# Dilated attention on one NeuronCore: the modulation's products in groups of four array quarters, and a score pair's two heads in alternation

## The chip, the cores and the metric

The kernel runs on one core of a Trainium2 chip as one program of five engines that run beside each other: TensorE (PE, with its weight loads shown as PEld), VectorE (DVE), ScalarE (ACT), GpSimd (POOL) and SyncE (SP), which here only issues DMA transfers. Each engine works through its own list of instructions in order and waits at semaphores for the others. The metric is the device time of one execution in microseconds (us). An execution that the hardware profiler records is taken apart from the timed ones.

## What is computed

One encoder layer, applied with the same weights to a request of 1024 rows and one of 256 rows (1280 together, model width 1024, all in float32). What matters here, from the reference:

```python
mod = jnp.einsum('bd,de->be', jax.nn.silu(c), ada_w) + ada_b
sh1, sc1, gt1, sh2, sc2, gt2 = jnp.split(mod, 6, axis=-1)
h = rmsnorm(x, norm1_g) * (1 + sc1[:, None]) + sh1[:, None]
z = jnp.einsum('bsd,de->bse', h, w_in)
...
for g, (window, dilation) in enumerate(DIL_CONFIGS):
    o_g, lse_g = dilated_group_attention(qkv[:, :, 0, hs], qkv[:, :, 1, hs], qkv[:, :, 2, hs],
                                         slopes[hs], window, dilation)
```

The modulation is a product of two conditioning vectors (one for each request) of length 1024 with a weight of 1024 x 6144. The dilated attention has three groups of four heads, each head 64 wide.

## The kernel before

The program is built in stages that follow each other: the first third of the modulation and the normalised input (to about 60 us), the products of the input with `w_in` by a seven-product scheme (line 244, to about 395 us), then the stage that the change touches ("c" in the code, about 395 to 794 us), then rope, values and the second branch's output ("psB", to about 890 us), latent attention, the output projections and the feed-forward part. A framework's scheduler decides in which order each engine gets its instructions and where it waits; the source gives it priorities, buffer rings and data flow. A tile with `tag` and `bufs` is a ring: a new tile of that tag waits until the oldest one's last reader is done.

Stage c goes through six steps, one for each pair of heads (two) in each group (three). A step has ten blocks `i` of 128 queries. For each block, `weights(i)` computes the scores of the pair's two heads, head 0 from partitions 0 to 63 of the query and key tiles and head 1 from partitions 64 to 127, each into its own bank of PSUM (`S0`, `S1`). In groups 0 and 1 a number is split in a high and a low part (`qh`, `ql`, `kh`, `kl`) and a score is the sum of three products (lines 823 to 825); in group 2 it is one product (line 827). DVE adds the bias and takes the row's extreme (line 832), ACT exponentiates (837), `outputs(i)` transposes on PE (847), copies, and multiplies with the values (862).

Three generators are woven into the ten blocks. `filler` (`side`) makes the remaining products with `w_in` (line 100), long runs of full-array products that need little of the other engines. `norms` (`side2`) normalises the latents. `modulation` (`side3`) makes the other two thirds of the modulation: eight chunks of 512 columns, each of eight products with contraction 128, 32 output rows (two are used) and 512 columns. Product k of a chunk writes quarter k % 4 of the bank `AD` (`tile_position=(0, 32 * j)`), so the four quarters of the array's columns serve four products. In the trace such a product is two PE rows, since a float32 product is made in two passes:

```python
w = mk(cpl, [P, 512], tag="ad", bufs=3)
nc.sync.dma_start(out=w, in_=ada_w[k * P:(k + 1) * P, 512 * c:512 * c + 512])
nc.tensor.matmul(ps[32 * j:32 * j + 32, :], lhsT=cT[:, k, :], rhs=w, start=(k < 4), stop=(k >= 4), tile_position=(0, 32 * j))
yield
```

The first third of the modulation (`ada_chunk`, line 167) has products of the same shape, issued eight in a row. The value rows of an attention group are loaded by `values` into a ring `v` of `VB` tiles with two blocks each; the next group's first blocks are loaded ahead.

Of the kernel before, what the change touches and what calls it, by code (L numbers as in the profile page):

```python
# [8 lines left out]
F32 = mybir.dt.float32  # L9
F32R = mybir.dt.float32r  # L10
# [6 lines left out]
P = 128  # L17
# [29 lines left out]
def kernel(  # L47
# [258 lines left out]
    def bank(tag, bufs=1):  # L306
        return mk(psC[1], [P, 512], tag=tag, bufs=bufs)
# [191 lines left out]
    close_pool(scm)  # L499


    VB, SB = 9, 7
    ccm = open_pool("c", "left")
    cpl = ccm[1]
    psC = open_pool("psC", space=PSUM)
    cT_, abT_ = mk(cpl, [P, KD, 32]), mk(cpl, [P, 6 * KD])
    nc.vector.tensor_copy(cT_, cT)
    nc.vector.tensor_copy(abT_, abT)
    cT, abT = cT_, abT_

    def cls(ap, g, i):
        if i < NS:
# [123 lines left out]
    def norms():  # L636
# [43 lines left out]
        for c, (c0, n) in enumerate(CH):  # L680
# [10 lines left out]
            nc.sync.dma_start(out=f32(kr_d)[1, 0:32, cs_], in_=f32(lo))  # L691
            yield

    NORM = 0, 1
    def modulation():
        for c in range(4, 12):
            ps = bank("AD")
            for k in range(KD):
                j = k % 4
                w = mk(cpl, [P, 512], tag="ad", bufs=3)  # L700
                nc.sync.dma_start(out=w, in_=ada_w[k * P:(k + 1) * P, 512 * c:512 * c + 512])
                nc.tensor.matmul(ps[32 * j:32 * j + 32, :], lhsT=cT[:, k, :], rhs=w, start=(k < 4), stop=(k >= 4), tile_position=(0, 32 * j))
                yield
            rows = stile()
            nc.scalar.copy(out=rows, in_=ps)
            tp = pp().rearrange("p (b n) -> p b n", b=4)
            for b in range(4):
                nc.tensor.transpose(tp[:, b, :], rows[:, b * P:(b + 1) * P], ident)
            chunk_cols(c, tp)
            yield  # L710
# [76 lines left out]
    for pair, g in steps:  # L787
        split = g < 2
        (qh, ql), (kh, kl) = qk[pair, g]
        nxt = steps.index((pair, g)) + 1  # L790
        more = queries_keys(*steps[nxt], qk[steps[nxt]]) if nxt < len(steps) else last_steps()
        if pair and g < 2:
            values(g + 1, 0, 6)
        if g == 0:
            bt = [mk(cpl, [P, 384], tag="bs", bufs=4) for _ in range(2)]
            for h in range(2):
                nc.sync.dma_start(out=bt[h], in_=bias0[2 * pair + h])
            btab = {0: bt, 1: bt}
        else:
            w = 384 if g == 1 else P  # L800
            btab = {}
            for q, src in enumerate((bias1s, bias1p) if g == 1 else (bias2s, bias2p)):
                if g == 1:
                    btab[q] = [mk(cpl, [P, 384], tag="bs", bufs=4) for _ in range(2)]
                else:
                    both = mk(cpl, [P, 384], tag="bs", bufs=4)
                    btab[q] = [both[:, P * h:P * h + P] for h in range(2)]
                for h in range(2):
                    nc.sync.dma_start(out=btab[q][h][:, 0:w], in_=src[2 * pair + h])
        nt = rtile()  # L810
        stat = mk(cpl, [P, 40], tag="stat", bufs=2)
        vg = vts[g]
        def weights(i):
            w0, o, blocks = window(g, i)
            wn = 256 if split else P
            q0 = P * i
            ps = [bank(f"S{h}") for h in range(2)]
            for h in range(2):
                hs = slice(64 * h, 64 * h + 64)
                dst = ps[h][:, 0:wn]  # L820
                if split:
                    a, b_ = qh[hs, q0:q0 + P], kh[hs, w0:w0 + wn]
                    nc.tensor.matmul(dst, lhsT=a, rhs=b_, start=True, stop=False)
                    nc.tensor.matmul(dst, lhsT=a, rhs=kl[hs, w0:w0 + wn], start=False, stop=False)
                    nc.tensor.matmul(dst, lhsT=ql[hs, q0:q0 + P], rhs=b_, start=False, stop=True)
                else:
                    nc.tensor.matmul(dst, lhsT=qh[hs, q0:q0 + P], rhs=kh[hs, w0:w0 + wn], start=True, stop=True)
            sb = stile()
            for h in range(2):
                bias = btab[0 if i < NS else 1][h]  # L830
                b0 = P - o if split else 0
                nc.vector.tensor_tensor_reduce(
                    out=sb[:, 256 * h:256 * h + wn], in0=ps[h][:, 0:wn], in1=bias[:, b0:b0 + wn],
                    scale=-0.125, scalar=3e38, op0=ALU.add, op1=ALU.min, accum_out=stat[:, 10 * h + i:10 * h + i + 1])
            for h in range(2):
                e = sb[:, 256 * h:256 * h + wn]
                nc.scalar.activation(out=e, in_=e, func=AF.Exp, scale=-1.0, bias=stat[:, 10 * h + i:10 * h + i + 1],
                                     accum_out=stat[:, 20 + 10 * h + i:21 + 10 * h + i])
            return sb, blocks

        def outputs(i, sb, blocks):
            tp = mk(psC[1], [P, 512], tag="PT", bufs=2)
            pt = stile()
            for bi, (b, off, m) in enumerate(blocks):
                for h in range(2):
                    cc = 256 * bi + P * h
                    nc.tensor.transpose(tp[0:m, cc:cc + P], sb[:, 256 * h + off:256 * h + off + m], ident)
            if all(m == P for _, _, m in blocks):
                nn = 256 * len(blocks)
                if i % 2:  # L850
                    nc.vector.tensor_copy(pt[:, 0:nn], tp[:, 0:nn])
                else:
                    nc.scalar.copy(out=pt[:, 0:nn], in_=tp[:, 0:nn])
            else:
                for bi, (b, off, m) in enumerate(blocks):
                    nc.vector.tensor_copy(pt[0:m, 256 * bi:256 * bi + 256], tp[0:m, 256 * bi:256 * bi + 256])
            oo = bank("O")[:, 0:P]
            for bi, (b, off, m) in enumerate(blocks):
                for h in range(2):
                    hs = slice(64 * h, 64 * h + 64)  # L860
                    vc = P * pair + 64 * h
                    nc.tensor.matmul(oo[hs, :], lhsT=vg[b][0:m, vc:vc + 64],
                                     rhs=pt[0:m, 256 * bi + P * h:256 * bi + P * h + P],
                                     start=(bi == 0), stop=(bi == len(blocks) - 1), tile_position=(0, 64 * h))
            if i % 2:
                nc.scalar.copy(out=cls(nt, g, i), in_=oo)
            else:
                nc.vector.tensor_copy(cls(nt, g, i), oo)

        quota = 0.0  # L870
        nxt_w = weights(0)
        for i in range(NT):
            now, nxt_w = nxt_w, weights(i + 1) if i + 1 < NT else None
            for part in range(2):
                quota += SIDE / 20
                while quota >= 1:
                    quota -= 1
                    next(side, None)
                if part == 0:
                    outputs(i, *now)  # L880
                if part == 0 or i % 2:
                    next(side3, None)
            for _ in range(SPEED if nxt == len(steps) else 1):
                next(more, None)
            if steps.index((pair, g)) >= NORM[0]:
                for _ in range(NORM[1]):
                    next(side2, None)
        nts[pair][g] = nt
        ps = pp()
        nc.tensor.transpose(ps[0:40, 0:P], stat, ident)  # L890
        srow = stile()[0:40, 0:P]
        nc.vector.tensor_copy(srow, ps[0:40, 0:P])  # L892
        nc.sync.dma_start(out=st_d[pair, g].rearrange("s h (i q) -> (s h i) q", q=P), in_=srow)
        run(more)
        if pair and g < 2:
            values(g + 1, 6)
    run(side2)
    run(side3)

# [59 lines left out]
    def rope_q(j, w):  # L959

        wh, wl = w
        for c, (c0, n) in enumerate(CH):
            ps = pb()
            mm3(ps[:, 0:n], wh, wl, [t[:, c0:c0 + n] for t in cqH], [t[:, c0:c0 + n] for t in cqL])
            tiles_ = vtile(), vtile(), mk(cpl, [P, 512], F32R, tag="ad", bufs=3), mk(cpl, [P, 512], F32R, tag="qk", bufs=3)
            half = rope(ps[:, 0:n], c, co_t[:, c0:c0 + n], si_t[:, c0:c0 + n], [t[:, 0:n] for t in tiles_])
            yield
            next(half)
            for s, t in enumerate(next(half)):
                nc.scalar.dma_start(out=f32(qr_d)[s, P * j:P * j + P, c0:c0 + n], in_=f32(t))  # L970
# [1000 lines left out]
```

## Time and profile before

| | |
|---|---|
| time, median of 3 runs | 2502.05 us (2501.76 to 2503.14) |
| the profiled execution's own time | 2507.67 us |
| its span in the profile | 2505.9 us |
| PE busy in the span | 2396.6 us (96%) |
| stage c, the six steps | about 417 to 736 us |
| stage c, what is left of the filler, and the merge | about 736 to 794 us |
| PE busy on line 702 | 61.8 us |

The profile gives the start and length of every instruction. PE products are pipelined: the length of one reaches past the start of the next, so what a product costs PE is read from its start to the next one's start, not from its length. The span leaves out 1.8 us of the profiled execution's own time.

### The profile page before, as it was taken

The page shows a single profiled execution, that of the slowest core. Times are in us where ns is not written, and L with a number is a line of the kernel's source. Part 1 is how long each engine was busy: PE and PEld are TensorE (multiplying, and loading weights), DVE is VectorE, ACT ScalarE, POOL GpSimd, SP SyncE. Part 2 cuts the span into 40 slices and gives each one's busy share as a digit, 9 for nine tenths or more (in the row PEclk, how much of TensorE's full clock was granted, in tenths as well). Part 3 has the DMA queues.
Part 4 walks back from the last instruction along what each step waited for, and adds up shares of the span by engine and source line. Part 5 has one row for each costly group of instructions (what it writes and reads, how often), then busy time and mean ns, then how long its engine had stood idle before and what let it go on. Part 6 is the DMA issues. An engine that isn't in the chain of part 4 may idle for free. (4 is left out here: it accounts for less than half of the span.)

```text
span 2505.9 us, 37001 instructions
## 1 busy us (share of the span) xinstructions
PE 2396.6 (96%) x13177; PEld 2006.3 (80%) x13177; DVE 1508.6 (60%) x2469; ACT 1081.3 (43%) x2106; POOL 1114.5 (44%) x802
## 2 busy tenths in 40 slices
PE   7899999999999899999998999988999999999987
PEld 3799997565568777777775778778999999988876
DVE  5733333433444778888888543466665566567768
ACT  4421113544433457777776443343322233254434
POOL 1443331100114336666668442045556555538473
PEclk9999999999989999999999989998999999999999
DMA  7132225556537953333333664332223223267554
GB/s 260 47 132 95 95 93 182 165 177 207 169 98 219 299 178 83 81 91 85 84 96 101 159 203 130 135 110 85 85 92 104 80 80 102 76 230 246 171 188 158
DMA packets 274771, 342.87 MB, mean 137 GB/s; under 512 B 24398, under 2 KB 177759, under 8 KB 274587
## 3 DMA queue, kind: packets, MB, share of 16 engines
q1 hardware_dynamic: 248942, 311.40, 40.3%
q10 hardware_dynamic: 25644, 29.12, 3.3%
q8 instruction: 103, 1.69, 0.3%
q14 instruction: 82, 0.66, 0.1%
HBM read 237.06 MB, written 94.19 MB: 132 GB/s over the span
## 5 line engine op out<-in xcount | busy, mean ns | idle before, releaser
L244 PE MATMUL X<-t,wh 128*128 128x320 f32 x2864 | 540.4, 311 | 9.7 <-ACT wh L230 5.7
L244 PEld LDWEIGHTS X<-t,wh 128*128 128x128 f32 x2864 | 453.0, 189 | 10.6 <-ACT wh L230 5.9
L81 POOL TENSOR_TENSOR pl<-p,ph 128x512 fp32r<-128x512 f32 x224 | 298.0, 1339 | 135.8 <-ACT ph L1127 110.3
L244 PE MATMUL X<-t,wl 128*128 128x320 f32 x1432 | 328.8, 311 | 6.3 <-DVE wl L78 6.3
L244 PEld LDWEIGHTS X<-t,wl 128*128 128x128 f32 x1432 | 241.0, 189 | 7.2 <-DVE wl L78 6.7
L1126 ACT ACTIVATE p<-S 128x512 f32<-128x512 f32 x272 | 163.5, 601 | 104.9 <-issue 39.6
L100 PE MATMUL pp<-t,wh 128*128 128x512 f32 (+3 forms) x672 | 201.7, 381 | 3.7 <-DVE sm L892 3.1
L81 POOL TENSOR_TENSOR wl<-wr,wh 128x512 fp32r<-128x512 f32 (+2 forms) x50 | 62.9, 1258 | 310.7 <-ACT wh L209 281.2
L1108 DVE TENSOR_REDUCE m<-mi 128x1 f32<-128x512 f32 x256 | 174.1, 686 | 34.8 <-PE mi L1107 32.0
L230 ACT CAST wh<-wr 128x512 fp32r<-128x512 f32 x113 | 70.3, 622 | 273.4 <-PE X L244 186.7
L78 DVE TENSOR_TENSOR ut<-X,ut 128x640 f32<-128x640 f32 x126 | 101.6, 821 | 138.4 <-PE X L244 85.8
L81 POOL TENSOR_TENSOR wl<-R,wh 128x512 fp32r<-128x512 f32 x63 | 103.4, 1642 | 145.1 <-ACT wh L230 145.1
L1127 ACT ACTIVATE ph<-S 128x512 fp32r<-128x512 f32 x272 | 162.6, 598 | 1.1 <-issue 0.3
L1796 PE MATMUL Y<-bh,ah 128*128 128x512 f32 x385 | 151.9, 395 | 7.5 <-DVE ut L78 6.6
L100 PEld LDWEIGHTS pp<-t,wh 128*128 128x128 f32 (+1 forms) x672 | 111.7, 185 | 58.0 <-issue 29.7
L1796 PE MATMUL Y<-bl,ah 128*128 128x512 f32 x385 | 152.1, 395 | 6.3 <-POOL bl L81 6.3
L1796 PE MATMUL Y<-bh,al 128*128 128x512 f32 x385 | 151.7, 394 | 0.0
L78 DVE TENSOR_TENSOR wl<-wr,wh 128x512 fp32r<-128x512 f32 x119 | 110.9, 932 | 52.7 <-ACT wh L230 47.7
L244 PE MATMUL X<-R,wh 128*128 128x320 f32 x736 | 138.2, 309 | 0.0
L78 DVE TENSOR_TENSOR pt<-X,pt 128x640 f32<-128x640 f32 x60 | 48.6, 824 | 135.9 <-PE X L244 84.5
L78 DVE TENSOR_TENSOR al<-ar,ah 128x640 fp32r<-128x640 f32 x75 | 89.5, 1195 | 57.0 <-ACT ah L1770 54.1
L100 PE MATMUL pp<-t,wl 128*128 128x512 f32 (+3 forms) x336 | 123.2, 367 | 0.0
(439 smaller groups left out, 5788.9 us busy)
## 6 DMA issues: line engine op xcount, KB each, us to landing
ac_d<-ut SPq DMA_DIRECT2D x77, 320.0 KB
ar<-ac_d SPq DMA_DIRECT2D x75, 320.0 KB
R<-in_w_up_dram SPq DMA_DIRECT2D x84, 256.0 KB
br<-in_w_down_dram SPq DMA_DIRECT2D x77, 256.0 KB
ad<-in_ada_w_dram SPq DMA_DIRECT2D x64, 256.0 KB
wr<-in_w_in_dram SPq DMA_DIRECT2D x48, 256.0 KB
rw<-in_w_in_dram SPq DMA_DIRECT2D x20, 512.0 KB
V<-v_d SPq DMA_DIRECT2D x16, 640.0 KB
```

The lines of the kernel that those rows point to most:

```text
L78: nc.vector.tensor_tensor(out=out, in0=a, in1=b, op=op)
L81: nc.gpsimd.tensor_tensor(out=out, in0=a, in1=b, op=op)
L100: nc.tensor.matmul(ps, lhsT=w[k], rhs=x[k], start=(k == 0 and w is wh and x is xh), stop=(k == n - 1 and w is wl))
L230: nc.scalar.copy(out=h, in_=a)
L244: nc.tensor.matmul(ps[:, z, 0:320], lhsT=a[:, k, :], rhs=b[q][k][:, 320 * z:320 * z + 320], start=(j == 0 and i == 0), stop=(j == n - 1 an ...
L1108: nc.vector.reduce_max(out=m2[:, i, c:c + 1], in_=ps, axis=AX.X)
L1126: nc.scalar.activation(out=p_, in_=ps, func=AF.Exp, scale=MSCALE)
L1127: nc.scalar.activation(out=ph, in_=ps, func=AF.Exp, scale=MSCALE)
L1796: nc.tensor.matmul(ps, lhsT=a[:, P * j:P * j + P], rhs=b, start=(f == 0 and a is ah and b is bh), stop=(f == HF - 1 and a is al))
```

## The change

The eight products of a chunk are now issued in two groups of four: four weight tiles are loaded first, and their four products, one for each quarter of the array's columns, follow each other in the code. The ring `ad` has four buffers instead of three. The score products of a block go term by term, head 0 and head 1 in turn, instead of three terms of head 0 and then three of head 1. Space for the fourth `ad` buffer comes from the ring `v` (8 tiles instead of 9) and from two small copies (`cT_`, `abT_`) that are dropped, the originals being used. Of the next group's value blocks four instead of six are loaded ahead.

```diff
-    VB, SB = 9, 7
+    VB, SB = 8, 7
...
-    cT_, abT_ = mk(cpl, [P, KD, 32]), mk(cpl, [P, 6 * KD])
-    nc.vector.tensor_copy(cT_, cT)
-    nc.vector.tensor_copy(abT_, abT)
-    cT, abT = cT_, abT_
...
+    def ad_tile(dt=F32):
+        return mk(cpl, [P, 512], dt, tag="ad", bufs=AD)
...
+    AD = 4
     def modulation():
         for c in range(4, 12):
-            ps = bank("AD")
+            ps, ws = bank("AD"), []
             for k in range(KD):
                 j = k % 4
-                w = mk(cpl, [P, 512], tag="ad", bufs=3)
+                w = ad_tile()
                 nc.sync.dma_start(out=w, in_=ada_w[k * P:(k + 1) * P, 512 * c:512 * c + 512])
-                nc.tensor.matmul(ps[32 * j:32 * j + 32, :], lhsT=cT[:, k, :], rhs=w, start=(k < 4), stop=(k >= 4), tile_position=(0, 32 * j))
+                ws.append(w)
                 yield
+                if j < 3:
+                    continue
+                for i in range(4):
+                    nc.tensor.matmul(ps[32 * i:32 * i + 32, :], lhsT=cT[:, k - 3 + i, :], rhs=ws.pop(0), start=(k < 4), stop=(k >= 4),
+                                     tile_position=(0, 32 * i))
...
-            values(g + 1, 0, 6)
+            values(g + 1, 0, 4)
...
-            for h in range(2):
-                hs = slice(64 * h, 64 * h + 64)
-                dst = ps[h][:, 0:wn]
-                if split:
-                    a, b_ = qh[hs, q0:q0 + P], kh[hs, w0:w0 + wn]
-                    nc.tensor.matmul(dst, lhsT=a, rhs=b_, start=True, stop=False)
-                    nc.tensor.matmul(dst, lhsT=a, rhs=kl[hs, w0:w0 + wn], start=False, stop=False)
-                    nc.tensor.matmul(dst, lhsT=ql[hs, q0:q0 + P], rhs=b_, start=False, stop=True)
-                else:
-                    nc.tensor.matmul(dst, lhsT=qh[hs, q0:q0 + P], rhs=kh[hs, w0:w0 + wn], start=True, stop=True)
+            terms = ((qh, kh), (qh, kl), (ql, kh)) if split else ((qh, kh),)
+            for t, (a, b_) in enumerate(terms):
+                for h in range(2):
+                    hs = slice(64 * h, 64 * h + 64)
+                    nc.tensor.matmul(ps[h][:, 0:wn], lhsT=a[hs, q0:q0 + P], rhs=b_[hs, w0:w0 + wn], start=(t == 0), stop=(t == len(terms) - 1))
```

How the scheduler sets these instructions is seen in its lists. First PE's list of before, in the first step of group 0, which is the place at which the trace stands at 425.4 us: line 823 to 825 are the three terms, `S_610` is head 0's bank, `S_611` head 1's, `R` the query and key tiles, and line 702 is a modulation product.

```order
L823 MATMUL S_610_3775<-R_3686,R_3672 128x256
L824 MATMUL S_610_3775<-R_3687,R_3672 128x256
L825 MATMUL S_610_3775<-R_3686,R_3673 128x256
L823 MATMUL S_611_3776<-R_3686,R_3672 128x256
L824 MATMUL S_611_3776<-R_3687,R_3672 128x256
L825 MATMUL S_611_3776<-R_3686,R_3673 128x256
L702 MATMUL AD_3802<-ad_3913,t_3651 32x512
L702 MATMUL AD_3802<-ad_3977,t_3651 32x512
```

Head 0's three terms stand ahead of head 1's three. Two modulation products stand next to each other here; of the 64, most stand alone, as in this piece of PE's list in the second step (line 847 transposes, line 862 multiplies with values, line 100 is the filler):

```order
L847 MATMUL PT_4625<-t_60,sm_4562 128x128 x4
L702 MATMUL AD_4476<-ad_4638,t_3651 32x512
L862 MATMUL O_4632<-sm_4626,v_3661 64x128 x2
L862 MATMUL O_4632<-sm_4626,v_3664 64x128 x2
L100 MATMUL pp_4653<-t_132,wh_4643 128x512
L100 MATMUL pp_4653<-t_140,wh_4643 128x512
L100 MATMUL pp_4653<-t_132,wl_4644 128x512
L100 MATMUL pp_4653<-t_133,wh_4643 128x512
L100 MATMUL pp_4653<-t_141,wh_4643 128x512
L100 MATMUL pp_4653<-t_133,wl_4644 128x512
L702 MATMUL AD_4476<-ad_4660,t_3651 32x512
```

In PE's list of the changed kernel, the same chunk's second half and the scores behind it (line 707 is now the modulation product, line 827 the score product):

```order
L707 MATMUL AD_4469<-ad_4631,t_100 32x512
L707 MATMUL AD_4469<-ad_4652,t_100 32x512
L707 MATMUL AD_4469<-ad_4694,t_100 32x512
L707 MATMUL AD_4469<-ad_4744,t_100 32x512
L827 MATMUL S_839_4771<-R_3983,R_3808 128x256
L827 MATMUL S_840_4772<-R_3983,R_3808 128x256
L827 MATMUL S_839_4771<-R_3984,R_3808 128x256
L827 MATMUL S_840_4772<-R_3984,R_3808 128x256
L827 MATMUL S_839_4771<-R_3983,R_3809 128x256
L827 MATMUL S_840_4772<-R_3983,R_3809 128x256
```

The four products of a group stand together, and the heads alternate. Counted over the whole list, the 64 modulation products stand in 58 unbroken runs before and in 29 in the changed kernel. There the first chunk's eight still stand almost one by one (seven runs), and the other 14 groups are cut in eight places, six times by value products (line 862) alone. Of the 40 blocks with three terms, all six score products stand unbroken in 29 blocks before and in 29 blocks in the changed kernel. Of the 20 blocks with one term the two products stand together in 15 before and in 13 in the changed kernel.

SP's list, where the four loads of the same chunk's first half stand (`qk` and `v` are other loads of this stage). Before:

```order
L701 DMA ad_4477<-in_ada_w_dram 128x512
L701 DMA ad_4531<-in_ada_w_dram 128x512
L565 DMA qk_4486<-qk_d 128x256
L565 DMA qk_4546<-qk_d 128x512
L701 DMA ad_4541<-in_ada_w_dram 128x512
L554 DMA v_4861<-vn_d 128x256
L645 DMA qk_4551<-lt_d 128x512
L554 DMA v_4861<-vn_d 128x256
L565 DMA qk_4595<-qk_d 128x512
L645 DMA qk_4599<-lt_d 128x512
L701 DMA ad_4586<-in_ada_w_dram 128x512
```

And in the changed kernel:

```order
L561 DMA qk_4536<-qk_d 128x512
L550 DMA v_4851<-vn_d 128x256 x2
L641 DMA qk_4541<-lt_d 128x512
L701 DMA ad_4470<-in_ada_w_dram 128x512
L701 DMA ad_4523<-in_ada_w_dram 128x512
L701 DMA ad_4532<-in_ada_w_dram 128x512
L701 DMA ad_4576<-in_ada_w_dram 128x512
L561 DMA qk_4584<-qk_d 128x512
```

The four loads, spread among others before, now follow each other; the four buffers of the ring come free together when the group ahead has been multiplied. From the end of stage psB on, each engine's list is the same in both kernels but for buffer numbers; PE's is the same from the last filler products of stage c on.

## Rows read from the trace of the kernel before

**Rows 1.** Page, part 1: busy us, share of the span, instructions of each engine.
```profile
PE 2396.6 (96%) x13177; PEld 2006.3 (80%) x13177; DVE 1508.6 (60%) x2469; ACT 1081.3 (43%) x2106; POOL 1114.5 (44%) x802
```

**Rows 2.** Windows: busy PE, PEld, DVE, ACT, POOL, then PEclk, DMA share, GB/s.
```profile
417.00:736.00 319.00, 313.76 (x1724) 186.42 (x1725) 129.20 (x446) 140.88 (x397) 32.83 (x28) 0.96 0.56 170
736.00:794.00 58.00, 57.63 (x309) 49.71 (x308) 22.71 (x33) 14.68 (x25) 13.67 (x8) 1.00 0.60 172
794.00:890.00 96.00, 86.98 (x458) 73.02 (x458) 75.20 (x135) 44.10 (x97) 40.15 (x34) 0.95 0.87 285
```

**Rows 3.** Groups of PE by form, 417 to 736 us.
```profile
L702 PE MATMUL AD<-ad,t 128*32 128x512 f32 x128 | 61.8, 609 | 3.4 <-DMA ad<-in_ada_w_dram 3.4
```

**Rows 4.** Timeline of PE, first step: start us, length us, line, count.
```profile
425.43 0.39 PE L823 MATMUL S<-R,R 64*128 64x256 f32 x2
425.65 0.29 PE L824 MATMUL S<-R,R 64*128 64x256 f32 x2
425.77 0.28 PE L825 MATMUL S<-R,R 64*128 64x256 f32 x2
425.98 1.05 PE L702 MATMUL AD<-ad,t 128*32 128x512 f32 x4
426.97 0.38 PE L823 MATMUL S<-R,R 64*128 64x256 f32 x1
...
427.51 0.30 PE L847 MATMUL PT<-t,sm 128*64 128x128 f32 x1
427.74 0.38 PE L823 MATMUL S<-R,R 64*128 64x256 f32 x1
...
428.29 0.52 PE L847 MATMUL PT<-t,sm 128*64 128x128 f32 x3
```

**Rows 5.** Timeline of PE, around two modulation products that stand alone.
```profile
457.47 0.28 PE L100 MATMUL pp<-t,wl 128*32 128x256 f32 x1
457.58 0.40 PE L100 MATMUL pp<-t,wh 128*32 128x256 f32 x2
...
460.52 0.30 PE L100 MATMUL pp<-t,wl 128*32 128x256 f32 x1
460.75 1.04 PE L702 MATMUL AD<-ad,t 128*32 128x512 f32 x2
461.73 0.44 PE L862 MATMUL O<-sm,v 64*64 64x128 f32 x4
```

**Rows 6.** Timeline of PE, stage a: modulation products of the same shape in a row.
```profile
26.78 1.06 PE L167 MATMUL S<-v,t 128*32 128x512 f32 x6
...
36.37 1.91 PE L167 MATMUL S<-v,t 128*32 128x512 f32 x12
```

**Rows 7.** Waits, 417 to 736 us: us in total, times, longest.
```profile
PE AD L702 <- DMA ad<-in_ada_w_dram: 3.4, 1, 3.4
...
PE pp L100 <- DVE sm L892: 3.1, 1, 3.1
...
SPq L701 <- PE AD L702: 91.6, 47, 6.3
```

**Rows 8.** Timelines of SP and PE: the first modulation loads, and their first product.
```profile
412.76 0.91 SPq L701 DMA_DIRECT2D ad<-in_ada_w_dram  x2
...
417.36 2.14 PE L702 MATMUL AD<-ad,t 128*32 128x512 f32 x4 [3.41 <-DMA ad<-in_ada_w_dram]
```

**Rows 9.** The tile ad: issues of its loads, ns min/median/max.
```profile
L701 SPq DMA_DIRECT2D ad<-in_ada_w_dram x64: 327/333/441, 412.8 to 670.5; - x64
```

**Rows 10.** Timeline of PE around the longest wait between the steps.
```profile
691.70 0.40 PE L100 MATMUL pp<-t,wl 128*128 128x512 f32 x1
695.25 1.22 PE L100 MATMUL pp<-t,wh 128*128 128x512 f32 x2 [3.15 <-DVE sm L892]
```

**Rows 11.** Windows: the 20 us with that wait, columns as in rows 2.
```profile
690.00:710.00 20.00, 16.85 (x61) 10.13 (x60) 6.10 (x30) 5.44 (x22) 0.76 (x1) 0.66 0.08 22
```

**Rows 12.** Line 507: the larger of the two copies, ns min/median/max.
```profile
L507 DVE COPY t<-t x1: 1153/1153/1153, 398.6 to 398.6; 128x256 f32<-128x256 f32 x1
```

More of the change, by code (lines that the diff above doesn't have):

```diff
@@ L895 @@
         if pair and g < 2:
-            values(g + 1, 6)
+            values(g + 1, 4)
     run(side2)
@@ L964, in rope_q @@
             mm3(ps[:, 0:n], wh, wl, [t[:, c0:c0 + n] for t in cqH], [t[:, c0:c0 + n] for t in cqL])
-            tiles_ = vtile(), vtile(), mk(cpl, [P, 512], F32R, tag="ad", bufs=3), mk(cpl, [P, 512], F32R, tag="qk", bufs=3)
+            tiles_ = vtile(), vtile(), ad_tile(F32R), mk(cpl, [P, 512], F32R, tag="qk", bufs=3)
             half = rope(ps[:, 0:n], c, co_t[:, c0:c0 + n], si_t[:, c0:c0 + n], [t[:, 0:n] for t in tiles_])
```

## The prediction

> **What bounds the kernel now.** I began with the page's busy shares. PE is busy 96% of the span [rows 1], but that is an average over stages, so I went on to windows around the stage that the change touches. In the six attention steps, 417 to 736 us, PE is busy 313.8 of 319 us, while ACT has 140.9 and DVE 129.2, and the DMA engines work at a share of 0.56 [rows 2]. No other engine is near its limit, and PE idles 5.2 us in all; the list of waits names two larger pieces of it, 3.4 us ahead of the first modulation product and 3.1 us behind a DVE copy [rows 7]. What is left of the filler, to 794 us, is PE again: 57.6 of 58 us. The stage behind it is different: PE idles 9 of 96 us there and DMA stands at 0.87 [rows 2]. So PE time that is saved inside the steps should come off the end of the steps nearly one to one, as long as PE isn't made to wait for something new. The third view was the groups of PE by form: the modulation, line 702, has 128 rows (64 products of two passes each) and covers 61.8 us [rows 3]. The fourth was the timeline, for what products cost from start to start.
>
> **The modulation's products.** A product that stands alone holds PE for 0.98 us: it starts at 460.75 and the next product at 461.73 [rows 5]. Two that stand together hold it for 0.99 us: 425.98 to 426.97, four rows where the lone one has two [rows 4]. The second product costs next to nothing, since it runs in another quarter of the array. Whether four do as well is seen in the first stage, whose products have the same shape: six rows (three products) last 1.06 us, and twelve rows (six products, so at least two rounds over four quarters) last 1.91 us [rows 6]. That is about 0.9 us a round. So the price goes by unbroken runs, not by products: 58 runs before, 29 after, both counted in PE's lists. 29 runs fewer at 0.98 us are 28.4 us; the 35 additional products that now ride along cost at most 0.01 us each (0.99 less 0.98), 0.3 us. A lone product also lengthens its neighbour: a filler product of 256 columns takes 0.11 us to the next start (457.47 to 457.58), but 0.23 us with a modulation product behind it (460.52 to 460.75) [rows 5]. Where a value product would have stood behind the filler anyway, I grant that none of this is won; between 0 and 0.12 us a run, I take 0.07, which is 2 us. Together -30.1 us.
>
> **The scores.** The edit makes heads 0 and 1 alternate, so that one head's product can run beside the other's, each in half of the array's rows. The trace says that they do so already. The program's order at 425.4 us is three terms of head 0, then three of head 1; the timeline shows both first terms at 425.43, both second terms at 425.65 and both third ones at 425.77, and all six are over at 425.98, after 0.55 us [rows 4]. PE pulled head 1's products ahead of head 0's later ones. Only where something else stands between the heads do they run apart: 426.97 to 427.51 and 427.74 to 428.29, 0.54 and 0.55 us, 1.09 in all [rows 4]. What counts is again how many blocks are unbroken, and that is 29 of 40 before and 29 after. The 11 others are cut elsewhere, which could be worth some 0.1 to 0.2 us each either way; of the one-term blocks two more are cut, at no more than the 0.54 us of a separate head each. I take 0, between -2 and +2 us.
>
> The Trainium skill, "TensorE: Matmul & The Clock Gate", section "Part 3: Packing small matmuls", says that matmuls start and end strictly in program order and that only weight loads are pulled ahead. By that rule the 29 blocks would not have overlapped before, and alternation would bring them from 1.09 to 0.55 us: 15.7 us more. The rows just quoted speak against it, and I go by the rows.
>
> **New waits of a group.** A group of four can only start when its fourth tile has landed, and its loads can only be issued when the group ahead has released the ring. Issuing takes 0.33 us each [rows 9]. The first load was issued at 412.76 and its product, which waited for it, ran at 417.36: 4.6 us [rows 8]. The last of four thus lands between 4.6 + 3 x 0.33 = 5.6 us after the release (if the transfers don't slow each other) and about 10.5 us: 256 KB at the rate of the steps' whole traffic, 170 GB/s at a share of 0.56 [rows 2], are 0.86 us of all engines' time, and 0.44 of them are free, so 2 us each for three more. I take 7.5 us, nearer to the lower end, since the 4.6 us were measured with DMA busier than its mean. What PE has to do meanwhile: the steps' list from the first modulation product to the last has about 880 other rows in 263 us less 57 us for the 58 runs, 0.23 us a row. Between the first and the second group of a chunk stand 45, 51, 47, 34, 46, 30 and 38 rows, 7.0 to 11.9 us; between chunks 53 to 76 rows, 12 us and more. At 7.5 us one group waits, 0.5 us; at 10.5 us three groups wait, 7.8 us together; at 5.6 us none. I add 2 us, because SP may come to the four loads late: it now spends 91.6 us waiting for the ring [rows 7], and whatever it waits for goes ahead of the loads.
>
> **The rest.** The two dropped copies are 1.2 us of DVE and less [rows 12], at 398.6 us, while PE works at the filler and later waits for a load, not for them: 0. Hidden by DVE's 60% of idle time, they would cost the 1.3 us without it. Four value blocks ahead instead of six: block 4 is first needed in the fifth block of a step, some 20 us after the step begins (319 us are 60 blocks of 5.3 us), and its load is issued at the step's start and takes 5 to 10 us as above: 0, at most 3 us if it were late once. One `v` tile less and one `ad` tile more in the stage behind, which is limited by DMA: I take +1 us, between -2 and +4.
>
> **Sum.** Against the profiled execution's 2507.7 us: -30.1 + 0 + 2 + 1 = -27.1, so 2480.6. That execution is 5.6 us above the median of the timed ones, 2502.05, so for these I forecast 2475.
>
> **Rivals.**
> (a) The groups wait, and the clock falls with them: slower. PE's one wait of 3.15 us inside the steps was followed by a stretch at the lower of the two levels: 690 to 710 us has a mean granted clock of 0.66 [rows 10, 11], which is 13.7 us at 1.2 GHz and 6.8 us lost beside the wait. A group that waits as long could cost 10 us. Three such waits eat the gain, and if all seven second groups did so the time would be 2502 - 30 + 70 = 2542. For it speaks that no load can run ahead of the release any more; against it that only three of these groups are closer than 10.5 us to the one ahead. 5%.
> (b) Half of the gain is lost: as the steps get shorter, other hand-overs end last (bias, exponent, transpose, copy of a block, whose engines have 40% to 44% of their time in use), or SP holds up weight loads of the filler behind the four. 15 us lost gives 2490. 14%.
> (c) The scores gain too: if the 29 unbroken blocks had taken 1.09 us before, alternation would give 29 x 0.54 = 15.7 us more, 2459. Against it stands the 0.55 us of [rows 4]; for it only that I show one block. 4%. (It is what the order rule of the page named above would make of the edit.)
> (d) The 3.15 us wait and its slow stretch at 692 us vanish with the new order: 10 us more, 2465. 9%.
> (e) Groups of four don't overlap, or as much is lost as won: within 5 us of 2502. 4%.
>
> **The numbers.** My forecast, with its own range of 2469 to 2484 by the bounds above, has 64%. Faster by over 0.2% (5 us, about what a measurement of this kernel can tell from no change) are the forecast, (b), (c) and (d): 91%; same 4%, slower 5%. The range leaves out (a), (e) and part of (c) and (b): 2461 to 2494.
>
> **What would show it.** In the profile after, modulation rows in runs of eight that last about 1 us; PE's time on them near 29 us where it was 57; three-term blocks still at 0.55 us; the last modulation product and the end of the steps some 27 us earlier, and every later stage as long as before. I'm wrong if PE waits for `ad` loads often, if the granted clock falls more often inside the steps, or if the stage behind takes back what the steps give.

## The result, and the profile after

| | before | changed |
|---|---|---|
| median (lowest to highest), 4 runs each | 2502.18 us (2501.76 to 2503.14) | 2468.85 us (2467.15 to 2471.0) |
| the profiled execution's own time | 2507.67 us | 2468.41 us |

The ratio is 0.9867 with a 95% interval of 0.985 to 0.9884: 33.3 us less by the medians. The prediction was 2475, 6 us above that; the measured time lies just below the prediction's own range, 2469 to 2484.

The page's first part for the changed kernel (columns as in [rows 1]):

```profile
PE 2355.0 (95%) x13177; PEld 1994.2 (81%) x13177; DVE 1502.2 (61%) x2467; ACT 1080.5 (44%) x2106; POOL 1109.5 (45%) x802
```

PE has as many instructions as before and is busy for 41.6 us less; DVE has the two copies less. The windows show where, for the six steps, the rest of the filler and the stage behind (about the same places in the program as in [rows 2], at earlier times):

```profile
418.00:704.00 286.00, 277.66 (x1741) 181.70 (x1742) 128.47 (x447) 140.07 (x398) 33.79 (x28) 0.98 0.62 189
704.00:761.00 57.00, 55.67 (x290) 47.30 (x288) 20.88 (x31) 14.62 (x25) 13.01 (x8) 1.00 0.59 173
761.00:842.00 81.00, 74.02 (x410) 62.70 (x410) 63.17 (x116) 41.19 (x87) 38.97 (x32) 1.00 0.93 307
```

The steps are about 33 us shorter, PE's busy time in them falls by 36 us, and what PE idles grows from 5.2 to 8.3 us. The stage behind is cut at other ends here, so not to be compared length for length; in the trace it takes 81.3 us from its first product to the start of latent attention, where it took 83.0, and DMA is still near its limit. The groups of PE in the steps, by form, with busy time, mean ns of one, and idle time ahead of them:

```profile
L862 PE MATMUL O<-sm,v 128*64 128x128 f32 x368 | 34.1, 294 | 4.7 <-DVE sm L851 3.8 <-ACT sm L853 0.8
...
L707 PE MATMUL AD<-ad,t 128*32 128x512 f32 x128 | 31.1, 604 | 1.7 <-DMA ad<-in_ada_w_dram 1.7
...
L827 PE MATMUL S<-R,R 64*128 64x256 f32 x240 | 30.5, 326 | 0.0
```

The modulation, line 707, covers 31.1 us where [rows 3] had 61.8, with as many rows. The timeline shows what a group costs; one row is a run of like products, and the next row's start tells when PE is free again:

```profile
475.10 0.60 PE L847 MATMUL PT<-t,sm 128*128 128x128 f32 x4
475.46 0.71 PE L100 MATMUL pp<-t,wh 128*128 128x512 f32 x2
...
478.06 1.06 PE L707 MATMUL AD<-ad,t 128*32 128x512 f32 x8
479.06 0.62 PE L827 MATMUL S<-R,R 64*128 64x256 f32 x6
479.61 0.73 PE L100 MATMUL pp<-t,wh 128*128 128x512 f32 x2
...
480.75 0.44 PE L713 MATMUL pp<-t,sm 128*128 128x128 f32 x2 [0.41 <-ACT sm L710]
...
494.60 0.60 PE L847 MATMUL PT<-t,sm 128*128 128x128 f32 x4
495.13 1.06 PE L707 MATMUL AD<-ad,t 128*32 128x512 f32 x8
496.12 0.72 PE L100 MATMUL pp<-t,wh 128*128 128x512 f32 x2
```

Eight rows, four products, hold PE from 495.13 to 496.12: 0.99 us, as one product did in [rows 5]. A block of six score rows takes 479.06 to 479.61, 0.55 us, as in [rows 4]. And four transposes take 0.36 us when filler follows (475.10 to 475.46) but 0.53 when a modulation product follows (494.60 to 495.13).

The waits in the steps (total us, times, longest), first PE's, then one of SP's queue:

```profile
PE O L862 <- DVE sm L851: 3.8, 4, 2.1
...
PE AD L707 <- DMA ad<-in_ada_w_dram: 1.7, 1, 1.7
PE pp L648 <- POOL sm L81: 1.5, 1, 1.5
PE pp L713 <- ACT sm L710: 1.3, 3, 0.7
...
SPq L701 <- PE AD L707: 24.9, 20, 4.6
```

The groups wait for their loads once only, at the first group. The 3.1 us behind line 892 of [rows 7] are gone, but new waits have come: above all, the value products now wait for DVE's copy of the transposes.

### The profile page after: what moved, and what is told of

It is laid out like the page before. It is cut to its first block, busy times and chain, and to the rows that moved or that the text cites. A ratio compares the mean times of both kernels' runs of the same rounds, so it can differ in the third digit from the quotient of the medians.

```text
span 2466.6 us, 36993 instructions
## 1 busy us (share of the span) xinstructions
PE 2355.0 (95%) x13177; PEld 1994.2 (81%) x13177; DVE 1502.2 (61%) x2467; ACT 1080.5 (44%) x2106; POOL 1109.5 (45%) x802
## 4 chain that ended last, share of the span: by engine, by line
PE 76%; DVE 8%; DMA 5%; issue 5%; POOL 4%; ACT 2%; SPq 1%; ACTq 0%; DVEq 0%; POOLq 0%
PE X L244 31%; PE Y L1796 7%; PE pp L100 7%; PE mi L1077 3%; PE mi L1107 2%; PE S L1173 2%; PE S L1172 2%; PE S L1174 2%; PE O L1211 2%; PE O L1210 2%; PE X L92 2%; PE X L94 2%; PE X L93 2%; POOL t L81 1%; PE X L467 1%
## 5 line engine op out<-in xcount | busy, mean ns | idle before, releaser
L1126 ACT ACTIVATE p<-S 128x512 f32<-128x512 f32 x272 | 163.6, 601 | 105.4 <-issue 38.5
```

The source lines that it names most:

```text
L1126: nc.scalar.activation(out=p_, in_=ps, func=AF.Exp, scale=MSCALE)
```

## Where the time went, summed over the trace

To compare kernels, every PE row from the first filler product to the first product of the stage behind was counted from its start to the next row's start, less PE's idle time; the sums of rows of one kind stand below, in us. "Low clock" is the time in that stretch at which the granted clock showed the lower of its two levels (1.2 instead of 2.4 GHz); its cost is spread over the other columns. The last column is from the start of latent attention to the start of PE's last row, where the program is the same in all. Each line is one profiled execution.

| kernel | stretch | PE idle | low clock | modulation | scores | transposes | last column |
|---|---|---|---|---|---|---|---|
| before | 395.5 | 8.3 | 23.9 | 57.8 | 39.8 | 25.8 | 1619.1 |
| changed | 360.5 | 11.0 | 10.2 | 29.2 | 38.3 | 20.7 | 1614.6 |
| groups alone | 358.0 | 12.0 | 0 | 29.3 | 39.1 | 20.0 | 1625.8 |
| scores alone | 388.1 | 4.9 | 17.1 | 57.3 | 38.3 | 25.6 | 1620.7 |
| one quarter | 375.6 | 5.2 | 0 | 58.2 | 36.0 | 19.3 | 1618.9 |
| supporting edits alone | 384.2 | 4.4 | 6.8 | 57.3 | 38.5 | 25.3 | 1618.6 |
| groups of two | 368.5 | 8.2 | 10.2 | 41.7 | 37.2 | 21.5 | 1621.0 |
| ring `v`, second time | 387.3 | 5.6 | 10.2 | 57.7 | 38.6 | 25.2 | 1618.7 |
| rope loads by ACT | 385.9 | 6.0 | 6.8 | 57.4 | 37.7 | 25.5 | 1620.3 |
| group in reverse order, second time | 347.7 | 11.3 | 6.8 | 17.1 | 38.2 | 20.7 | 1619.3 |

## The experiments

Ratios are to the kernel before on the same chip and in the same stretch of runs, with 95% intervals. Every kernel computes what the kernel before computes; e3 leaves out the sum over the quarters because its products accumulate in one quarter already.

### e1: the groups without the score order

The changed kernel with the score loop of before (three terms of head 0, then three of head 1).

> The change without its second part: modulation in groups of four, score products in the old order (three terms of head 0, then three of head 1). In PE's list the 64 modulation products stand in 29 unbroken runs, as in the changed kernel. Theory of runs (a run costs 0.98 us whether it holds one product or four, scores already overlap): all of the gain, 2502 - 33 = 2469, within 4 us; modulation rows take PE about 29 us. Rival (alternating scores carry part of it): 2477 to 2485.

Measured: 2473.11 us, 0.9869 (0.9852 to 0.9887). The groups and what supports them bring all of the gain.

### e2: the score order without the groups

The kernel before with

```diff
-            for h in range(2):
...
+            for t, (a, b_) in enumerate(terms):
+                for h in range(2):
```

> The kernel before with the score products of the two heads in alternation, nothing else. 58 runs of modulation products. Theory of runs: nothing, 2502 within 3 us, and three-term blocks take 0.55 us as before. Rival (PE works strictly in order, alternation is what lets the heads overlap): 2502 - 16 = 2486.

Measured: 2501.9 us, 0.999 (0.9978 to 1.0003). No gain is shown, and surely not 16 us: 15.7 of 2506 would be 0.994.

### e3: groups of four, but all in one quarter

```diff
-                    nc.tensor.matmul(ps[32 * i:32 * i + 32, :], ..., start=(k < 4), stop=(k >= 4), tile_position=(0, 32 * i))
+                    nc.tensor.matmul(ps[0:32, :], ..., start=(k < 4 and i == 0), stop=(k >= 4 and i == 3), tile_position=(0, 0))
...
```

Loads, ring and groups are the same, and the products stand in 27 runs instead of 29. What differs is the quarter of the array and, behind a chunk, that its copy and its transposes have 32 rows instead of 128, as the edit's other lines have it.

> The changed kernel, but all eight products of a chunk go to the first quarter of the array and add up there, so that a group of four can't run side by side (the sum over quarters afterwards is left out, being done by the accumulation; transposes of 32 rows). 27 unbroken runs. Theory (the gain is the overlap of quarters): 64 products at about 0.86 us and 27 switches at 0.12 us, 58 us instead of 29: 2469 + 29 = 2498, that is about the time before. Rival (grouping gains by fewer switches, or by fewer waits, and not by the quarters): 2469 to 2475.

Measured: 2492.77 us, 0.9952 (0.9936 to 0.9969). Its groups of PE and its timeline:

```profile
L707 PE MATMUL AD<-ad,t 128*32 128x512 f32 x128 | 60.0, 597 | 0.8 <-DMA ad<-in_ada_w_dram 0.8
```

```profile
475.81 3.62 PE L707 MATMUL AD<-ad,t 128*32 128x512 f32 x8
479.36 0.62 PE L829 MATMUL S<-R,R 64*128 64x256 f32 x6
```

The eight rows that took 0.99 us take 3.55 us, and the modulation is back at 60.0 us: it is the quarters that make the products ride along, not the grouping. But 12 of the 33 us stayed, which the theory had not allowed for: something besides the modulation's own rows gains. Some 7 us are what the supporting edits bring by themselves (e4, next); beyond these the table shows the transposes, 19.3 us against 25.3 in e4, with 27 runs of modulation products instead of 58.

### e4: the supporting edits without groups and score order

The changed kernel with one load and one product at a time as before, and the scores of before; four `ad` buffers, eight `v` tiles, four value blocks ahead, no copies.

> Only the supporting edits: four buffers in the ring ad, eight tiles in the ring v, four value blocks ahead, the two copies dropped; modulation products one by one, scores in the old order. 58 runs, PE's list as before. Theory: nothing, 2502 within 3 us. Rival (the wait of 3.15 us with its slow stretch near 692 us, or the stage behind, changed by the rings and not by the groups): 2492 to 2497.

Measured: 2498.98 us, 0.9970 (0.9961 to 0.9979): some 7 us, where the theory had nothing. e1, in the same stretch of runs, differs from e4 by the groups alone and is 25.9 us faster. The place of the 7 us is sought in e6, e7, e9 and e12.

### e5: groups of two

```diff
-                if j < 3:
+                if j % 2 == 0:
                     continue
-                for i in range(4):
+                for i in (j - 1, j):
...
```

> The changed kernel with modulation products issued in groups of two instead of four. 42 unbroken runs in PE's list (58 before, 29 in the changed kernel). Theory of runs: 13 runs more than the changed kernel, at 0.98 us: 13 us slower than it, about 20 us faster than the kernel before on the same chip (ratio 0.992). Rival (what counts is that all four quarters are filled, or that a group of four loads arrives together): no gain beyond that of the supporting edits, ratio 0.997.

Measured: 2482.13 us, 0.9916 (0.9899 to 0.9934). 42 runs, and the modulation takes 41.7 us in the table: 0.99 us a run, as for 58 and 29 runs. The price goes by runs.

### e6: the kernel before without the two copies

```diff
-    cT_, abT_ = mk(cpl, [P, KD, 32]), mk(cpl, [P, 6 * KD])
...
-    cT, abT = cT_, abT_
```

> The kernel before without the two copies of the conditioning vectors, nothing else. The supporting edits together gained 7 us (ratio 0.997) where I had given them nothing. If the copies are what did it (they stood on DVE's path at the stage's start, and the first load and all that follows starts earlier): ratio 0.997. If not: 1.000 within 0.001.

Measured: 2506.63 us, 1.0009 (0.9996 to 1.0021). The copies are free, as predicted.

### e7 and e12: only the ring `v`

```diff
-    VB, SB = 9, 7
+    VB, SB = 8, 7
...
-            values(g + 1, 0, 6)
+            values(g + 1, 0, 4)
...
```

> The kernel before with eight tiles in the ring v and four value blocks loaded ahead instead of nine and six, nothing else. If fewer early value loads on SP's queue are what gained 7 us (loads of the key rotation near 690 us stand earlier, and PE's 3.15 us wait with its stretch at the lower clock goes): ratio 0.997, and the profile shows no clock drop near 690 us. If not: 1.000 within 0.001.

Measured: 2499.27 us, 0.9991 (0.9977 to 1.0006): by itself inconclusive. Its profile, though, had no drop of the clock at 690 us, so it was run again.

> The smaller ring v alone once more, beside the moved loads. If the shorter chain before the last step is worth what the profiles show (stage c 8 us shorter), the ratio is 0.997 in both; if the profiles of the kernel before are merely of its slower executions, both are between 0.998 and 1.000.

Measured: 2499.59 us, 0.9977 (0.9967 to 0.9986), some 6 us. By this second measurement fewer value tiles and a shorter look-ahead make the kernel faster; the first one doesn't exclude that they do nothing. That a fourth `ad` buffer alone would do it too wasn't tried, since without the space that the other edits free it has no room.

### e9: the wait at 690 us by another way

The kernel before, nothing changed but who issues the nine loads of the latents' rope (`kp_d`, cosine, sine):

```diff
             for d, src in ((x, kp_d[:, cs_]), (co, rope_cos[0:32, cs_]), (si, rope_sin[0:32, cs_])):
-                nc.sync.dma_start(out=d, in_=src)
+                nc.scalar.dma_start(out=d, in_=src)
```

> The kernel before with the nine loads for the rotation of the latent key issued by ACT instead of SP, so that they don't stand behind SP's other loads. In the kernel before the last of them lands at 692.3 us, DVE waits 3.2 us for it, the copy of the statistics stands behind DVE's wait, and PE waits 3.15 us for that copy and then runs 13.7 us at the lower clock. If this chain is what the supporting edits shortened: that wait of PE falls below 1 us, no clock drop follows it, and the ratio to the kernel before is about 0.997, as with the supporting edits. If the gain of those edits lies elsewhere: the ratio stays at 1.000.

Measured: 2501.73 us, 0.9976 (0.9965 to 0.9988), 4.6 us by the medians. The place, in the kernel before, first on SP:

```profile
683.77 2.92 SPq L206 DMA_DIRECT2D wr<-in_w_in_dram  x2
...
688.00 0.39 SPq L685 DMA_DIRECT2D sm<-kp_d  x1
```

One of SP's waits ahead of it, and the window of 2 us from its issue (columns as in [rows 2]):

```profile
SPq L206 <- POOL wl L81: 2.0, 1, 2.0
```

```profile
688.00:690.00 2.00, 2.00 (x14) 1.24 (x13) 1.05 (x4) 0.14 (x1) 0.00 (x0) 1.00 0.87 263
```

And DVE:

```profile
688.67 0.42 DVE L851 COPY sm<-PT 128x256 f32<-128x256 f32 x1
692.26 0.01 DVE L624 LOAD_MASK_SELECT qk<-sm  x1 [3.17 <-DMA sm<-kp_d]
...
694.92 0.27 DVE L892 COPY sm<-pp 40x128 f32<-40x128 f32 x1
```

SP is taken up for 2.9 us by two other loads (`wr`, 256 KB each), 2.0 of them waiting for POOL before it can issue the second; only behind that does it issue the load of `kp_d`, while DMA is at a share of 0.87, and DVE sits 3.17 us before it. The small copy of line 892 stands behind that on DVE, and PE's filler waits 3.15 us for this copy [rows 10]; the clock falls as this wait ends and is at its lower level for 13.7 us [rows 11]. In the same place of e9, DVE, PE, and the window around it:

```profile
687.74 0.01 DVE L624 LOAD_MASK_SELECT qk<-sm  x1 [0.54 <-DMA sm<-kp_d]
...
690.73 0.27 DVE L892 COPY sm<-pp 40x128 f32<-40x128 f32 x1
```

```profile
691.05 0.73 PE L100 MATMUL pp<-t,wh 128*128 128x512 f32 x2 [0.87 <-DVE sm L892]
```

```profile
688.00:708.00 20.00, 18.97 (x114) 13.26 (x113) 12.84 (x57) 8.80 (x37) 1.14 (x2) 1.00 0.22 63
```

DVE's wait is 0.54 us, PE's 0.87, and the granted clock is 1.00 where it was 0.66; PE gets 114 rows done in 20 us instead of 61. In e4 the chain is short too; PE's row there, and the window:

```profile
690.58 0.73 PE L100 MATMUL pp<-t,wh 128*128 128x512 f32 x2 [0.93 <-DVE sm L892]
```

```profile
687.00:707.00 20.00, 19.07 (x112) 13.38 (x113) 12.45 (x58) 8.77 (x35) 1.39 (x2) 1.00 0.23 65
```

And in e12, on SP, the window of 2 us from the issue of `kp_d`, and DVE:

```profile
682.33 0.40 SPq L206 DMA_DIRECT2D wr<-in_w_in_dram  x1
...
687.34 0.60 SPq L685 DMA_DIRECT2D sm<-kp_d  x1
```

```profile
687.34:689.34 2.00, 2.00 (x14) 1.20 (x13) 0.91 (x5) 0.27 (x1) 0.00 (x0) 1.00 0.28 63
```

```profile
689.29 0.01 DVE L624 LOAD_MASK_SELECT qk<-sm  x1 [1.04 <-DMA sm<-kp_d]
```

Here one load of `wr` stands ahead of `kp_d` instead of two, DMA is at a share of 0.28 instead of 0.87, and DVE can go on 1.95 us after the issue, against 4.26 us before (688.00 to 692.26). The same place in all kernels with one product at a time, and in e5:

| kernel | loads of `wr` on SP just ahead of `kp_d` | PE's wait for line 892's copy, us | low clock that begins with it, us |
|---|---|---|---|
| before | 2 | 3.15 | 13.7 |
| e2 | 2 | 1.87 | 10.2 |
| e6 | 2 | 2.54 | 3.4 |
| e5 | 2 | 1.83 | 10.2 |
| e4 | 1 | 0.93 | 0 |
| e7 | 1 | 0.84 | 0 |
| e12 | 1 | 1.01 | 0 |
| e9 | `kp_d` issued by ACT | 0.87 | 0 |

In the table two loads ahead go with the long waits. e5 has the supporting edits and still two loads ahead, so these edits don't shorten the chain in every program. Two loads alone don't make the wait either: e8 and e11 have two as well, the changed kernel and e1 have one, and in none of the four does PE wait for the copy of line 892 there. By e9 the shortened chain is worth some 5 us, and by e4 and e12 the supporting edits bring about as much where the same chain is short. That the second load ahead is what makes `kp_d` late is read from the rows and argued, not tried by itself; e9 moves nine loads, so a gain of the other eight isn't excluded either.

### e8 and e11: the products of a group in reverse order; e10: the changed kernel again

```diff
-                for i in range(4):
-                    nc.tensor.matmul(..., rhs=ws.pop(0), ...)
+                for i in (3, 2, 1, 0):
+                    nc.tensor.matmul(..., rhs=ws[k - 3 + i], ...)
```

The group's first product now needs the tile that is loaded last, so that the scheduler has less cause to start a group and then cut it: 17 runs instead of 29.

> The changed kernel with each group's four products issued in reverse order, the last loaded tile's first. The scheduler then leaves 15 of the 16 groups whole: 17 unbroken runs instead of 29. Theory of runs: 12 runs fewer at 0.98 us: 12 us faster than the changed kernel, ratio about 0.982 to the kernel before. Rival (whole groups wait for their last load, now that none of a group can start early): as the changed kernel, 0.987, with waits of PE for loads of ad in the profile that the changed kernel doesn't have.

Measured: 2466.65 us, 0.9856 (0.9834 to 0.9878). The other two ran beside each other:

> The changed kernel once more, beside the two kernels that are compared with it on the same chip. Theory of runs and of the shortened chain together: 26 + 7 us faster than the kernel before, ratio 0.987.

> The groups in reverse order once more (17 unbroken runs instead of 29). Its profile shows stage c 12.6 us shorter than that of the changed kernel, of which 12.1 us are modulation products, but its measured ratio (0.9856) was hardly better. Theory of runs: beside the changed kernel on one chip it is 12 us faster (ratio 0.982). Rival (what stage c gives is taken back behind it, by stretches at the lower clock in stages that are the same in both): 0 to 4 us faster.

Measured: 2471.73 us, 0.9858 (0.9845 to 0.9871) for the changed kernel, and 2466.73 us, 0.9837 (0.982 to 0.9855) with the group in reverse order. It is the fastest version that ran, but the intervals overlap: 5 us by these medians, 2 us by e8 against the first runs. The modulation of e11 in the steps:

```profile
L707 PE MATMUL AD<-ad,t 128*32 128x512 f32 x128 | 18.1, 605 | 0.1
```

It went from 31.1 to 18.1 us, and the whole stretch in the table is 12.8 us shorter than the changed kernel's first profile (8.9 shorter than that of e10, which has 356.6). Less than that arrives at the end. The windows of what lies behind the stretch, to the end, are first the changed kernel's, then those of e1, e10 and e11 (PE's lists are the same there; e11's window holds 17 products more):

```profile
845.00:2466.60 1621.60, 1556.01 (x8315) 1349.03 (x8314) 1112.46 (x1618) 763.31 (x1378) 880.30 (x629) 0.98 0.41 124
```

```profile
841.70:2474.60 1632.90, 1563.36 (x8315) 1353.28 (x8314) 1115.80 (x1618) 763.54 (x1378) 882.89 (x629) 0.98 0.40 123
```

```profile
840.20:2469.30 1629.10, 1562.12 (x8315) 1352.83 (x8315) 1120.91 (x1618) 763.93 (x1379) 881.08 (x629) 0.98 0.40 124
```

```profile
829.50:2458.50 1629.00, 1561.46 (x8332) 1352.16 (x8330) 1123.38 (x1622) 766.16 (x1383) 884.55 (x629) 0.98 0.41 124
```

The same 8315 products take 1621.6 us in one execution of the changed kernel and 1629.1 in another, so 7 us come and go with no change to the program. A single profile therefore can't say what e11's 13 us of PE time are worth at the end; that stays open.

## Why the prediction was right, and where it was not

**The modulation's runs: right.** 28.4 us less 0.3 were forecast for 29 runs fewer; the table has 57.8 against 29.2, 28.6 us. Runs of 58, 42, 29 and 17 cost 57.8, 41.7, 29.2 and 17.1 us: one microsecond a run, whatever it holds up to four products. e3 shows that the quarters are the cause.

**The neighbours: mis-sized.** Taken as 2 us; the transposes alone fell by 5.1 us, and by 6.5 in e3, which has about as few runs but no products that ride along. The estimate was made from a filler product of 256 columns, 0.12 us a run and 0.07 on the mean. A transpose is dearer: four of them take 0.53 us ahead of a modulation product and 0.36 ahead of filler, 0.17 us more, in the rows above. In the trace of before 39 of the 58 runs stand right behind transposes, in the changed kernel's 11 of 29: 28 fewer at 0.17 us are 4.8 us.

**The scores: right.** 0 was forecast; e2 gave 0.999 with 1 inside its interval, and a block still takes 0.55 us. The Trainium skill, "TensorE: Matmul & The Clock Gate", section "Part 3: Packing small matmuls", has matmuls start and end strictly in program order. This case doesn't agree: [rows 4] shows head 1's first term beside head 0's, two places ahead of its turn in PE's list. e2 gained neither the prediction's 15.7 us nor the some 10 us that would be left if only head 0's last term and head 1's first could overlap (an estimate: five terms of 0.18 us instead of six, against three, in 29 blocks): its interval ends at 5.5 us. What was said ahead, that each engine works through its list in order, therefore doesn't hold for PE in this place.

**The new waits: mis-sized, and at another place.** 2 us were set down for groups that wait for their loads. They did so once, 1.7 us at the first group, which waited before as well [rows 7]; no second group of a chunk did. New waits came elsewhere: the value products wait for DVE's copy of the transposes (3.8 us in all), the modulation's own transposes for ACT's copy (1.3 us). In the table PE's idle time grows from 8.3 to 11.0 us only because two older waits have shrunk, the 3.15 us one and the one for the first load; against e4, where they have shrunk too, it grows from 4.4 to 11.0, by 6.6 us, and to 12.0 in e1. With less modulation work between them, PE reaches these hand-overs sooner; this reading is argued from the waits and not tested. A slip in the prediction's reading: of the 5.2 us that PE idles from 417 to 736 us, the 3.4 us ahead of the first modulation product are no part but for the last 0.36, since that wait ended at 417.36.

**The supporting edits: the step that was wrong.** Copies, ring and look-ahead were entered at 0 and +1; they brought some 7 us (e4). The prediction looked at what these edits could delay and not at what stands ahead of what on SP's queue. Rival (d), the end of the 3.15 us wait and of its slow stretch, therefore did not compete with the forecast but came beside it. It was sized at 10 us, 3.15 of the wait and 6.8 of the clock; e9, which took PE's wait to 0.87 us and had no drop there, measured 4.6 us by the medians. The drop is not as long in each execution: e2 and e6, which don't touch these loads, had waits of 1.87 and 2.54 us there and drops of 10.2 and 3.4 us.

**The other rivals.** (a) did not come: the granted clock in the steps went from 0.96 [rows 2] to 0.98. Of (b) a part came, 6.6 us of its 15 by the idle time against e4. (c) and (e) are ruled out by e2, and by e1 and e5.

**What was to be seen.** Modulation rows in runs of eight at about 1 us, near 29 us in all, and score blocks at 0.55 us are there. The last modulation product starts at 655.9 us instead of 680.4, 24.5 us earlier, and the steps end some 33 us earlier, 6 more than forecast, for the transposes and the chain at 690 us.

**The sum.** By this profile the stretch is 35.0 us shorter: 28.6 for the modulation, 5.1 for the transposes and 1.5 for the scores, less 2.7 of idle time, are 32.5; the other 2.5 lie in filler and value products, where the cost of the low clock shows (10.2 us of it against 23.9). That is near the 33.3 us of the medians; the part behind, which is 4.5 us shorter in this one profile, varies by more than that. e4 and e1 part the sum more cleanly, since they differ by the groups alone: the stretch falls by 26.2 us, 28.0 for the modulation and 5.3 for the transposes less 7.6 of idle time, with 0.5 us in the rest. With e4's 7 us that is the 33 us measured.

**Luck.** That the forecast is only 6 us off is in part luck: its terms were off by some 8 us for the supporting edits and 3 us for the neighbours in one direction, and by some 5 us for the new waits in the other.

## What to carry to other kernels

Small products that use one quarter of the array cost by the unbroken run, so they should be issued four to a run, and the code should make the first product of a group depend on the last load, so that a scheduler has no cause to cut it. Before two independent products are reordered to overlap, look in the timeline whether they already do. And when buffers or look-ahead change, read the DMA issuing queue for what now goes, or waits, ahead of a small load that a busy engine waits for.

## What the runs showed of the hardware that was not expected

One wait of PE of 3.15 us was followed by 13.7 us at 1.2 GHz [rows 10, 11], while waits of 0.84 to 1.01 us at the same place (e4, e7, e9, e12) were followed by none there. The length of the wait alone doesn't set the drop: 1.83 and 1.87 us (e5, e2) were followed by 10.2 us, 2.54 us (e6) by 3.4, and in the kernel before the 3.41 us of [rows 8] by 3.4.

A product's cost depends on what follows it: four transposes take 0.36 us ahead of full-array filler and 0.53 us ahead of a modulation product, which uses 32 of the array's columns.

PE started score products out of the order of its list: by the trace's single rows, head 1's first term 0.01 us behind head 0's, ahead of head 0's second and third [rows 4].

The part of the program behind the changed stage, the same in all kernels, took 1614.6 to 1625.8 us in the profiled executions of the table. Of two profiles of the changed kernel, the one with more time at 1.2 GHz in that part (73 us against 62) was the longer; that the clock is the cause is not shown.
